# A two-layer decoder trunk on one core: one weight pool for all layers, output projections through the seven-product pair, evacuations queued ahead of the casts that reuse a slot

## The chip, the cores and the metric

The kernel runs on 1 core of a Trainium2 chip. It is timed in device microseconds, from the start to the end of one execution, and the number that counts is the median of several runs. TensorE multiplies; VectorE and ScalarE prepare its operands and take its results; GpSimd does some elementwise work; the SyncE queue issues nearly all loads.

## The reference, cut to what matters

For a sequence of 256 positions and a width of 2048, two layers are computed in float32:

```python
for layer in range(2):
    h = rms_norm(x, mix_norm[layer])
    mix = ssd_mla_mixer(h, ...) if layer == 0 else stick_breaking_mixer(h, ...)
    x = x + mix
    h = rms_norm(x, ffn_norm[layer])
    x = x + (silu(h @ w_gate) * (h @ w_up)) @ w_down     # hidden width 5632
return rms_norm(x, final_norm)
```

The mixer of layer 0 is a Mamba-2 scan (SSD, 4 groups of 8 heads) beside latent attention (MLA, 4 groups of 4 heads). Their outputs, 2048 wide each, are joined and multiplied by one output matrix of 4096 x 2048. The mixer of layer 1 is stick-breaking attention (4 groups of 4 heads) with an output matrix of 2048 x 2048. Each of the three 2048 x 2048 products that end a mixer is called an output projection here: two in layer 0 (`uT` of the SSD, `oT` of MLA), one in layer 1 (`oT` of stick-breaking).

## The kernel before, in words

**Exact products.** TensorE multiplies in a reduced float32 format, so every operand is split into a high part (a cast on ScalarE, L251) and a low part (source minus high part, on VectorE, L252). A product is three matmuls: high x high, low x high, high x low. The activations stand transposed, 128 of the contraction at a time; a matmul has 128 rows and 512 columns. Weights arrive as tiles of 128 x 4 x 512 floats (1 MB), and splitting them is most of what VectorE and ScalarE do.

**Plain projection** (`project`, L337 to L363). For each of 4 column blocks of 512, over 16 contraction blocks and 2 halves of the sequence: 16 x 2 x 3 = 96 matmuls into two of four PSUM banks (L345 to L347). All input projections, the output projections and `w_down` run so.

**Seven-product pair** (`pair`, L470 to L556), for gate and up only. The first half of the contraction of two column blocks is done as a 2 x 2 block product with seven products instead of eight (sums of weight blocks at L470, sums of activation blocks in `block_operands`, L430 to L450, 12 matmuls each at L499, L500 and L504), the second half directly (L532 to L534). One running bank collects four of the seven products and is copied out between them (`keep`, L510; differences at L515). A pair has 7 x 12 + 96 = 180 matmuls, where two plain column blocks have 192. The eight weight tiles of a pair become eleven split parts, and four sums of 128 x 2048 are formed on VectorE.

**Buffers.** In the mixers ("acts" region) there are three weight tiles, and split parts of two contraction blocks (128 x 1024), four of each. In the FFN ("sums" region) there are four weight tiles, split parts of four contraction blocks (128 x 2048), three of each, and two tiles for sums. The two regions share one space, and `region` (L88) closes one before it opens the other, so the first split parts of an FFN reuse the space of the last parts and operands of a mixer. All else that is small comes from a pool of 42 tiles of 128 x 512 (`s2`).

**Order.** TensorE's instructions run in the order in which the program writes them. Side work (attention heads, transposes) is written as generators that say after how many ticks they go on; a tick passes with every six matmuls or so. On the other engines a scheduler fixes the order ahead of the run, by a priority number: casts of weights count up from 100000, adds to the residual and copies out of a running bank have 50000 (`URGENT`), most else ten million. Each engine then works through its queue in that order; an instruction that waits holds up those behind it.

**SSD groups** (`ssd_group`, L943 to L998). Each of the four groups transposes its part of x (L975), scales it (L976, L977), lets GpSimd form `xd` (L980) and after a `yield 3` has TensorE multiply it (L983). GpSimd also multiplies the decay masks (L967, four a group) and adds the last term of the group before (L998).

## Time and profile before

| what | value |
|---|---|
| median of 3 runs | 2491.4 us (2491.02 to 2493.19) |
| the profiled execution | 2491.61 us, span 2489.9 us, 28071 instructions |
| TensorE busy, matmuls | 2438.8 us, 98% of the span |
| VectorE busy | 1739.2 us, 70% |
| ScalarE busy | 1324.8 us, 53% |
| loaded from HBM | 450.85 MB, 182 GB/s over the span |

The profile is one execution. "Busy" is the time in which an engine had an instruction in work; matmuls overlap, so the rate at which they start says more than their busy time. "Idle before" is the time in which an engine stood still ahead of an instruction, with the releaser whose semaphore came last. The weight loads of TensorE (PEld) run under the matmuls. In the first 750 us lie the mixer of layer 0 and the first pairs of its FFN; this FFN ends near 1350 us, the stick-breaking mixer near 1764 us, and the FFN of layer 1 fills the rest.

### The profile page before, as it was taken

To read this page: it belongs to the slowest core of one execution; us is meant where nothing else is said; L and a number is where in the kernel's file an instruction comes from. 1 tells how busy PE (TensorE), PEld (TensorE's weight loads), DVE (VectorE), ACT (ScalarE), POOL (GpSimd) and SP (SyncE) were. 2 spreads that over 40 slices of the span, in tenths; PEclk is the share of its full clock that TensorE was granted. 3 is DMA by queue.
4 is the path that set the end of the run, shared out by engine and by line. 5 is a ranking of instruction groups with operands and counts; after the bars stand their busy time and mean duration, and the time that the engine had idled before them with its cause. 6 is when DMAs were issued, how large, how long until landed. Compare 5 with 4: busy or idle time off the path is not lost.

```text
span 2489.9 us, 28071 instructions
## 1 busy us (share of the span) xinstructions
PE 2438.8 (98%) x11176; PEld 2008.5 (81%) x11176; DVE 1739.2 (70%) x1631; ACT 1324.8 (53%) x1421; POOL 127.7 (5%) x165
## 2 busy tenths in 40 slices
PE   8989999999899999999999999999999999999998
PEld 7777887788778888888878888888778888888877
DVE  6776555546777878787984555556777878787874
ACT  6655555434554545454654456564554545554553
POOL 1342121000000000000000000000000000000001
PEclk9999999999999999999999999999999999999999
DMA  7554553355465656565654555555555656565653
GB/s 236 187 168 136 183 163 111 119 186 186 168 215 175 220 177 224 174 209 196 204 202 152 183 161 163 169 170 184 178 195 184 217 173 221 170 234 170 237 188 117
DMA packets 257828, 454.81 MB, mean 183 GB/s; under 512 B 20716, under 2 KB 45424, under 8 KB 257696
## 3 DMA queue, kind: packets, MB, share of 16 engines
q1 hardware_dynamic: 255168, 446.48, 54.3%
q0 software_dynamic: 1952, 5.48, 0.7%
q8 instruction: 88, 1.44, 0.2%
q10 hardware_dynamic: 576, 1.05, 0.1%
q14 instruction: 44, 0.36, 0.0%
HBM read 450.85 MB, written 2.13 MB: 182 GB/s over the span
## 4 chain that ended last, share of the span: by engine, by line
PE 60%; issue 34%; DVE 3%; POOL 1%; DMA 1%; ACT 1%; SPq 0%; POOLq 0%; ACTq 0%; DVEq 0%
PE acc L345 13%; PE acc L347 13%; PE acc L346 13%; PE acc L532 3%; PE acc L534 3%; PE acc L533 3%; PE acc L499 2%; PE acc L500 2%; PE acc L504 2%; DVE wl L252 1%; PE tr L261 1%; PE at L1062 1%; POOL s L967 1%; ACT wh L251 1%; PE at L991 1%
## 5 line engine op out<-in xcount | busy, mean ns | idle before, releaser
L252 DVE TENSOR_TENSOR wl<-w,wh 128x1024 fp32r<-128x1024 f32 (+2 forms) x586 | 997.7, 1709 | 553.1 <-ACT wh L251 549.1
L251 ACT CAST wh<-w 128x1024 fp32r<-128x1024 f32 (+2 forms) x586 | 837.1, 1430 | 788.2 <-PE acc L347 531.9
L345 PE MATMUL acc<-wh,s 128*128 128x512 f32 (+1 forms) x1728 | 692.2, 401 | 0.6 <-ACT wh L251 0.6
L346 PE MATMUL acc<-wl,s 128*128 128x512 f32 (+1 forms) x1728 | 671.5, 389 | 1.8 <-DVE wl L252 1.7
L347 PE MATMUL acc<-wh,s 128*128 128x512 f32 (+1 forms) x1728 | 672.4, 389 | 0.0
L347 PEld LDWEIGHTS acc<-wh,s 128*128 128x128 f32 x1728 | 325.4, 188 | 68.9
L346 PEld LDWEIGHTS acc<-wl,s 128*128 128x128 f32 x1728 | 326.5, 189 | 66.0 <-DVE wl L252 2.8
L345 PEld LDWEIGHTS acc<-wh,s 128*128 128x128 f32 x1728 | 326.4, 189 | 63.6 <-issue 2.4
L534 PE MATMUL acc<-wl,s 128*128 128x512 f32 x704 | 274.1, 389 | 0.0
L532 PE MATMUL acc<-wh,s 128*128 128x512 f32 x704 | 273.9, 389 | 0.0
L533 PE MATMUL acc<-wh,s 128*128 128x512 f32 x704 | 273.9, 389 | 0.0
L499 PE MATMUL acc<-wh,s 128*128 128x512 f32 x616 | 245.4, 398 | 0.0
L500 PE MATMUL acc<-wh,s 128*128 128x512 f32 x616 | 242.2, 393 | 0.0
L504 PE MATMUL acc<-wl,s 128*128 128x512 f32 x616 | 166.9, 393 | 12.3 <-DVE wl L252 12.3
L251 ACT CAST wh<-wsum 128x2048 fp32r<-128x2048 f32 x66 | 126.4, 1915 | 87.3 <-PE acc L533 33.7
L252 DVE TENSOR_TENSOR wl<-wsum,wh 128x2048 fp32r<-128x2048 f32 x66 | 150.7, 2286 | 13.5 <-ACT wh L251 13.5
L534 PEld LDWEIGHTS acc<-wl,s 128*128 128x128 f32 x704 | 132.1, 188 | 28.2 <-DVE wl L252 0.8
L533 PEld LDWEIGHTS acc<-wh,s 128*128 128x128 f32 x704 | 132.1, 188 | 27.4
L532 PEld LDWEIGHTS acc<-wh,s 128*128 128x128 f32 x704 | 132.1, 188 | 27.4
L504 PEld LDWEIGHTS acc<-wl,s 128*128 128x128 f32 x616 | 115.7, 189 | 39.2 <-DVE wl L252 15.3
L499 PEld LDWEIGHTS acc<-wh,s 128*128 128x128 f32 x616 | 117.8, 191 | 23.6
L500 PEld LDWEIGHTS acc<-wh,s 128*128 128x128 f32 x616 | 117.4, 191 | 23.5
(247 smaller groups left out, 2057.8 us busy)
## 6 DMA issues: line engine op xcount, KB each, us to landing
w<-in_w_gate_dram SPq DMA_DIRECT2D x88, 1024.0 KB, 5.1
w<-in_w_up_dram SPq DMA_DIRECT2D x88, 1024.0 KB, 5.1
w<-in_w_down_dram SPq DMA_DIRECT2D x88, 1024.0 KB, 5.0
w<-in_w_qkv_dram SPq DMA_DIRECT2D x48, 1024.0 KB, 5.0
w<-in_w_in_dram SPq DMA_DIRECT2D x47, 1024.0 KB, 5.1
w<-in_w_out_even_dram SPq DMA_DIRECT2D x32, 1024.0 KB, 4.9
w<-in_w_out_odd_dram SPq DMA_DIRECT2D x16, 1024.0 KB, 4.9
w<-in_w_ukv_dram SPq DMA_DIRECT2D x32, 256.0 KB, 3.8
```

The costliest lines, as they stand in the source:

```text
L251: nc.scalar.copy(hi, src)
L252: nc.vector.tensor_tensor(lo, src, hi.bitcast(F32), op=ALU.subtract)
L261: self.nc.tensor.transpose(pt[:, k, t * P:(t + 1) * P], src(t, 2 * k2 + k), self.ident)
L345: nc.tensor.matmul(ps[t], hi[:, ts], wh, start=k == 0, stop=False)
L346: nc.tensor.matmul(ps[t], hi[:, ts], wl, start=False, stop=False)
L347: nc.tensor.matmul(ps[t], lo[:, ts], wh, start=False, stop=k == nk - 1)
L499: mm(ps, hi[:, k], wh[:, k], start=start and k == 0, stop=False, skip_group_check=True)
L500: mm(ps, lo[:, k], wh[:, k], start=False, stop=False, skip_group_check=True)
L504: mm(ps, hi[:, k], wl[:, k], start=False, stop=k == 3, skip_group_check=True)
L532: mm(ps, hi, wh, start=False, stop=False, skip_group_check=True)
L533: mm(ps, lo, wh, start=False, stop=False, skip_group_check=True)
L534: mm(ps, hi, wl, start=False, stop=stop, skip_group_check=True)
```

## The change

1. **One weight pool.** Weight tiles (4) and split parts (3 of each, 128 x 2048) come from one pool in all layers. The shared space is left with `s2x` (8 tiles) and, from the SSD's output projection on, the two tiles for sums; it changes once, inside layer 0. Other tiles move to the pool of 42.
2. **Output projections through the pair.** `project_residual` replaces `project` and `add_residual`: two pairs for each output projection, each of which ends in adds to the residual. For the SSD the blocks 0 and 1 are made into seven operands by `operand_block`; for MLA and stick-breaking the head outputs of groups 0 and 1 are kept as unsplit blocks, from which `operand_ready` makes the operands. The signs of the sums change, the number of products and sums in a pair does not. Each bank's tile of a pair now runs its eight high-weight matmuls before its four low-weight ones. The first pair of MLA's and of stick-breaking's projection has the order `LATE`.
3. **Evacuations in the queue.** `urgent()` gives copies out of PSUM priority 50000 and notes them with the number of the part; the casts of a part three or more later are queued behind them (`after_urgent`).
4. **Ticks.** Several waits of the side work change: 3 to 6 in an SSD group, 6 to 7 and 3 to 4 in an MLA head, 2 to 8 and 4 to 8 elsewhere. The FFN's operands wait 15 ticks.

The core of the diff:

```diff
+    @contextmanager
+    def urgent(self):
+        traced = self.nc.cur_bb.bb.instructions
+        keep, self.tc.cur_priority = self.tc.cur_priority, self.URGENT
+        last = traced[-1]
+        yield
+        self.tc.cur_priority = keep
+        n = next(k for k in reversed(range(len(traced))) if traced[k] is last) + 1
+        self.pressing.extend((self.parts, ins) for ins in traced[n:]
+                             if ins.engine in (mybir.EngineType.Activation, mybir.EngineType.DVE))
+    def after_urgent(self):
+        order = ExitStack()
+        for part, ins in self.pressing:
+            if part <= self.parts - 3:
+                order.enter_context(self.tc.issue_after(ins))
+        self.pressing = [p for p in self.pressing if p[0] > self.parts - 3]
+        return order
...
-        return self.xp.tile([P, *shape], dt, name=self.nm("s2x"), tag="s2x", bufs=20)
-    def wtile(self):
-        self.wn += 1
-        pool, bufs = (self.xp, 1) if self.shared_kind == "sums" and self.wn % 4 == 0 else (self.wp, 3)
-        return pool.tile([P, 4, 512], F32, name=self.nm("w"), tag="w", bufs=bufs)
-    def part(self, tag):
-        nk, bufs = (2, 4) if self.shared_kind == "acts" else (4, 3)
-        return self.xp.tile([P, nk, 512], F32R, name=self.nm(tag), tag=tag, bufs=bufs)
+        return self.xp.tile([P, *shape], dt, name=self.nm("s2x"), tag="s2x", bufs=8)
+    def wtile(self, tag="w", dt=F32, bufs=4):
+        return self.wp.tile([P, 4, 512], dt, name=self.nm(tag), tag=tag, bufs=bufs)
+    def part(self, tag):
+        return self.wtile(tag, F32R, 3)
...
+    MIXED = ("M1", "M3", "M5", "M2", "M6", "M4", "M7", "c0", "c1", "c2", "c3")
+    LATE = ("M1", "M3", "M5", "M2", "M6", "c0", "M4", "M7", "c1", "c2", "c3")
+    def project_residual(self, st, view, scale=None, done=None, order=MIXED):
...
+        for n in (0, 2):
+            self.pair(st, view(n), view(n + 1), add(n), add(n + 1), self.MIXED if n else order)
+            if done:
+                done(n)
+                done(n + 1)
...
     def wsplit(self, w):
         wh, wl = self.part("wh"), self.part("wl")
-        with self.priority(self.wprio):
+        self.parts += 1
+        with self.priority(self.wprio), self.after_urgent():
...
     def stick(self, st):
...
-        for n in range(4):
-            ps = self.project(aT, self.cols(i["w_out_odd"][0], n * 512), KD)
-            self.add_residual(ps, n)
-            if n < 2:
-                self.operand_block(st, n, self.g_ffn[1])
-            else:
-                self.norm_block(st, n, self.g_ffn[1], rank=self.URGENT)
+        self.project_residual(oT, lambda n: self.cols(i["w_out_odd"][0], n * 512), None,
+                              lambda n: self.norm_next(st, n, self.g_ffn[1]), self.LATE)
...
         nc.gpsimd.tensor_tensor(v3(xd), v3(xdt[0]), bc(self.edec[:, 0, hs]), op=ALU.mult)
-        yield 3
+        yield 6
```

What it moves is shown at three places, each before and after. **GpSimd in the second SSD group**: `s_233` to `s_236` (after: `s_197` to `s_200`) are the masks, `s2x_185` (after: `s_30`) takes the last term of the group before, and the last row is `xd`.

```order
L967 TENSOR_TENSOR s_233_1194<-s_233_1194,s_182_918 128x512
L998 TENSOR_TENSOR s2x_185<-s2x_185,s_249_1318 128x512
L967 TENSOR_TENSOR s_234_1196<-s_234_1196,s_182_918 128x512
L967 TENSOR_TENSOR s_235_1198<-s_235_1198,s_184_932 128x512
L967 TENSOR_TENSOR s_236_1200<-s_236_1200,s_184_932 128x512
L980 TENSOR_TENSOR s_262_1397<-s2x_178,edec_819 128x512
```

```order
L1036 TENSOR_TENSOR s_197_1132<-s_197_1132,s_158_880 128x512
L1036 TENSOR_TENSOR s_198_1134<-s_198_1134,s_158_880 128x512
L1036 TENSOR_TENSOR s_199_1136<-s_199_1136,s_160_894 128x512
L1036 TENSOR_TENSOR s_200_1138<-s_200_1138,s_160_894 128x512
L1067 TENSOR_TENSOR s_30_185<-s_30_185,s_216_1280 128x512
L1049 TENSOR_TENSOR s_222_1327<-s2x_178,edec_789 128x512
```

Before, three of the four masks stand between the last term and `xd`; now all four stand ahead of both.

**VectorE where the stick-breaking mixer meets the FFN of layer 1.** Before, the last two adds to the residual and the first rows of the first FFN pair (`wsum` and `w` on the left are sums of weight tiles, `wl` low parts):

```order
L252 TENSOR_TENSOR wl_13101<-w_13094,wh_13100 128x1024
L401 TENSOR_TENSOR xres<-acc_12964,xres 128x512
L401 TENSOR_TENSOR xres<-acc_12965,xres 128x512
L470 TENSOR_TENSOR wsum_13150<-w_13134,w_13136 128x2048
L252 TENSOR_TENSOR wl_13153<-w_13134,wh_13152 128x2048
L470 TENSOR_TENSOR wsum_13156<-wsum_13150,w_13138 128x2048
L470 TENSOR_TENSOR w_13136<-w_13136,w_13138 128x2048
```

After, the end of the second pair of the output projection: `s_2180` to `s_2186` are low parts of the FFN's seven operands, `wl_12641` is the low part of the pair's last tile, `wl_12691` that of the first tile of the first FFN pair:

```order
L526 TENSOR_TENSOR wsum_12687<-w_12673,w_12671 128x2048
L269 TENSOR_TENSOR s_2180_12565<-s_2170_12545,s_2179_12564 128x512
L269 TENSOR_TENSOR s_2182_12569<-s_2171_12546,s_2181_12568 128x512
L526 TENSOR_TENSOR wsum_12688<-w_12675,wsum_12687 128x2048
L444 TENSOR_TENSOR s_2143_12387<-acc_12359,s_2143_12387 128x512
L269 TENSOR_TENSOR s_2184_12573<-s_2147_12402,s_2183_12572 128x512
L425 TENSOR_TENSOR xres<-s_2143_12387,xres 128x512
L444 TENSOR_TENSOR s_2167_12514<-acc_12360,s_2167_12514 128x512
L269 TENSOR_TENSOR s_2186_12577<-s_2172_12547,s_2185_12576 128x512
L425 TENSOR_TENSOR xres<-s_2167_12514,xres 128x512
L269 TENSOR_TENSOR wl_12641<-w_12346,wh_12640 128x2048
L269 TENSOR_TENSOR wl_12691<-w_12671,wh_12690 128x2048
```

The operands and two sums of the next pair now stand ahead of the last low part of the pair in work. From the row behind the first low part of this pair (`wl_12352`) up to and with `wl_12641` the queue has 42 rows: 14 of 128 x 2048 and 28 of 128 x 512.

**TensorE at the end of MLA's first output pair.** The last head's transposes (L1153) and its last product (L1159, L1160) stand close ahead of the tile that needs the head's split (`s_817` to `s_820`); before, its rows had a whole further projection (that of the SSD) behind them.

```order
L559 MATMUL acc_4470<-wh_4755,s_725_4076 128x512
L1159 MATMUL at_4779<-s_888_4742,s_815_4435 128x256
L1160 MATMUL at_4779<-s_888_4742,s_816_4437 128x128
L1153 MATMUL tr_4784<-ident,s_880_4698 128x128 x3
L559 MATMUL acc_4470<-wl_4756,s_722_4073 128x512 x2
L559 MATMUL acc_4470<-wl_4756,s_724_4075 128x512 x2
L1159 MATMUL at_4798<-s_894_4788,s_815_4435 128x256
L1160 MATMUL at_4798<-s_894_4788,s_816_4437 128x128
L559 MATMUL acc_4471<-wh_4794,s_817_4439 128x512
```

Four matmuls are left between the transposes and the product that needs their copy.

370 lines of the change are left out of this document (202 added, 168 removed).

## The prediction

> **What bounds the kernel now.** I read the busy shares first, then the chain of waits in order of time, then a table of stretches by stage, then who waited for whom.
>
> ```profile
> core 0 of [0], span 2489.9 us
> PE 2438.8 (98%) x11176; PEld 2008.5 (81%) x11176; DVE 1739.2 (70%) x1631; ACT 1324.8 (53%) x1421; POOL 127.7 (5%) x165
> ...
> 1911.46 0.91 PE acc L504 x4
> 1914.18 0.91 PE acc L504 x4
> ```
>
> TensorE is busy almost throughout. The last two rows give its rate: they are the ends of two products of 12 matmuls that follow one another in a steady FFN pair, 2.72 us apart, so 0.227 us a matmul. While it runs at that rate only fewer matmuls help. What else can be had lies where it does not, and the stretches show where. After the two ends of a stretch come its length, then busy time of TensorE, weight load, VectorE, ScalarE and GpSimd, then granted clock.
>
> ```profile
> 1906.80:1989.40 82.60, 82.60 (x369) 68.24 (x368) 69.80 (x43) 49.66 (x36) 0.00 (x0) 1.00 0.61 204
> 652.40:750.40 98.00, 88.72 (x380) 71.63 (x380) 83.81 (x60) 57.67 (x49) 0.00 (x0) 0.97 0.54 183
> 1764.30:1862.30 98.00, 89.64 (x377) 72.48 (x376) 83.28 (x59) 57.06 (x48) 0.00 (x0) 0.95 0.57 193
> 116.00:149.20 33.20, 29.84 (x153) 24.26 (x151) 26.60 (x45) 18.98 (x24) 16.54 (x13) 1.00 0.55 181
> 149.20:183.40 34.20, 30.84 (x149) 24.69 (x149) 23.75 (x43) 18.03 (x23) 13.30 (x11) 0.95 0.46 154
> 183.40:217.70 34.30, 30.94 (x149) 24.74 (x149) 23.74 (x43) 18.03 (x23) 13.27 (x10) 0.95 0.46 154
> 217.70:252.00 34.30, 34.30 (x160) 27.78 (x161) 15.69 (x25) 18.08 (x29) 2.20 (x1) 0.95 0.40 126
> ...
> PE acc L504 <- DVE wl L252: 12.3, 6, 3.4
> PE at L983 <- POOL s L980: 10.1, 3, 3.4
> PE tr L261 <- DVE s L575: 9.9, 4, 2.9
> PE acc L346 <- DVE wl L252: 1.7, 1, 1.7
> ```
>
> Two steady pairs take 82.6 us with no idle TensorE (first row). The first two pairs of either FFN take 98.0 us, with VectorE near its limit (83 us of work). In the SSD groups TensorE is idle 3.4 us a group and then runs at a clock of 0.95. The waits (total, times, longest) name both: low weight parts from VectorE at the FFN starts, and `xd` from GpSimd at L983. A wait costs more than itself, as two matmuls just behind one show:
>
> ```profile
> 1779.70 0.63 PE L500 MATMUL acc<-wh,s 128*128 128x512 f32 x1
> 1780.13 0.63 PE L499 MATMUL acc<-wh,s 128*128 128x512 f32 x1
> ```
>
> They start 0.43 us apart, about half the rate.
>
> **The change part by part.** *Fewer matmuls.* An output projection drops from 4 x 96 = 384 matmuls to 2 x 180 = 360; three of them save 72, at 0.227 us **16.3 us**. The rate is that of the same instruction in the FFN, so this term is firm as long as TensorE is fed.
>
> *SSD groups.* The idle times are 33.20 - 29.84, 34.20 - 30.84 and 34.30 - 30.94, in all 10.1 us; the three stretches at 0.95 lose 0.05 x 102.8 = 5.1 us. GpSimd's queue in one such group:
>
> ```profile
> 139.15 2.21 POOL L998 TENSOR_TENSOR s2x<-s2x,s 128x512 f32<-128x512 f32 x1 [0.76 <-DVE s L997]
> 141.33 5.74 POOL L967 TENSOR_TENSOR s<-s,s 128x512 f32<-128x512 f32 x3
> 147.02 2.02 POOL L980 TENSOR_TENSOR s<-s2x,edec 128x512 f32<-128x512 f32 x1
> ```
>
> The three masks between L998 and `xd` take 5.74 us and move ahead of L998; the queue needs to be only 3.4 us earlier. On TensorE I count 60 matmuls from the last product of a group to L983 of the next, before and after, so the longer `yield` alone gives nothing there and the order on GpSimd must do it. Bounds: 0 if the masks come late all the same, **15.2 us** if all goes; I take 15.2, since GpSimd was idle ahead of L998.
>
> *Region change after the first FFN.* The single wait at L346, 1.7 us, stands at the start of stick-breaking, where the old regions were exchanged. One pool removes it: **1.7 us** (0 to 1.7).
>
> *The FFN starts.* 98.0 against 82.6 is 15.4 us, of which some is the 16 transposes of the norm:
>
> ```profile
> 1950.45 0.60 PE tr L261 x4
> ...
> L252 DVE TENSOR_TENSOR wl<-w,wh 128x2048 fp32r<-128x2048 f32 x264 | 602.9, 2295 | 225.2 <-ACT wh L251 225.1
> L252 DVE TENSOR_TENSOR wl<-w,wh 128x1024 fp32r<-128x1024 f32 x310 | 386.6, 1249 | 319.5 <-ACT wh L251 315.6 <-DMA w<-in_w_uq_dram 1.6 <-DMA w<-in_w_ukv_dram 1.5
> ...
> 1777.69 2.28 DVE L252 TENSOR_TENSOR wl<-wsum,wh 128x2048 fp32r<-128x2048 f32 x1
> 1779.88 2.28 DVE L252 TENSOR_TENSOR wl<-w,wh 128x2048 fp32r<-128x2048 f32 x1
> ...
> 140.13 0.68 DVE L976 TENSOR_TENSOR s2x<-tr,dt 128x512 f32<-128x512 f32 x1
> 140.73 0.68 DVE L977 TENSOR_TENSOR s2x<-tr,hp 128x512 f32<-128x512 f32 x1
> ```
>
> At 0.60 us for four, 2.4 us; 13.0 us are lost at each start, 26 us together. Then the first split parts waited for the last tiles of the old region; that cause goes. But the load on VectorE moves forward into the new pairs. The second pair of an output projection has, from behind its first low part to its last, 42 rows on VectorE. Queued back to back the wide ones start 2.19 us apart and the short ones 0.60 us: 14 x 2.19 + 28 x 0.60 = 47.5 us. TensorE gets from the pair's start to the last tile's low part in 7 x 2.72 + 3 x 5.44 + 8 x 0.227 + 16 transposes 2.4 = 39.5 us. So VectorE ends 8.0 us late if both start together. It can be some 5 us ahead (three parts may be buffered), which leaves 3, and it can lose 4 us to waits for casts and loads, which makes 12; I take 9. In the first FFN pair the norm's splits add to a queue without lead: 0 to 5 us, I take 3. That is 12 a site, 3 to 17. At the old starts 9.28 and 8.36 idle us came with 2.9 and 4.9 us of lost clock (0.03 and 0.05 of 98), 0.44 a us; for shorter stalls I take a little less, so 14 us a site. Against the 13.0 that go: **+2 us** for the two sites, from -20 to +24.
>
> By a rule of the Trainium skill this factor would fall: "TensorE: Matmul & The Clock Gate", section "What's actually happening", says that the clock halves only after an idle window of about 3.4 us. If the new stalls are all shorter, a site costs 12 and, as an estimate by this page, the sum falls by 4 us. The row at 1779.70 came after waits of 3.4 and 1.9 us, so it does not decide that.
>
> *MLA's tail.* The last head's transposes are followed by four matmuls (0.9 us), then by the product that needs their copy, then by a tile that needs the split of that product:
>
> ```profile
> L1081 ACT COPY s<-tr 128x384 f32<-128x384 f32 x16 | 7.6, 474 | 0.0
> L251 ACT CAST s2x<-at 128x256 fp32r<-128x256 f32 x32 | 11.8, 370 | 9.1 <-PE at L1086 8.7 <-PE at L681 0.2
> L252 DVE TENSOR_TENSOR s2x<-at,s2x 128x256 fp32r<-128x256 f32 x32 | 13.4, 419 | 2.5 <-ACT s2x L251 2.0
> L251 ACT CAST wh<-w 128x2048 fp32r<-128x2048 f32 x264 | 504.8, 1914 | 433.1 <-PE acc L347 221.4 <-PE acc L533 109.0 <-issue 38.6
> ```
>
> Copy, cast and low part are 1.3 us, and each can find one wide cast ahead of it (1.9 us). Between 0.4 us (1.3 less the cover) and 6: **+3 us**.
>
> *The SSD's own pairs.* Here a pair has 15 wide rows and about 13 short ones: 32.9 + 7.8 = 40.7 us on VectorE against 180 x 0.227 = 40.8 on TensorE; 0 to 6, I take **+1.5 us**. The cover is the lead that VectorE brings from the input projections; without it both pairs lose about 3 each.
>
> *Wider casts.* In the mixers a cast on VectorE becomes 2.29 us long instead of 1.25, so an attention step can start 1.05 us later. An MLA head has one tick more at two such steps (six matmuls, 1.36 us each), which covers it there; I take **+2 us**, from 0 to 25 (8 groups with 3 such steps each). In all 302 of the shorter casts become 151 long ones, 0.2 us cheaper per pair, which VectorE has no use for off the path: nothing.
>
> Steady FFN pairs keep their counts and sizes: nothing, covered by 12.8 us of VectorE slack in two pairs.
>
> Sum: -16.3 - 15.2 - 1.7 + 2 + 3 + 1.5 + 2 = -24.7. From the span of 2489.9 that is 2465.2; the profiled execution took 2491.61, 1.7 more than its span, and the median is 0.2 below it: **2467 us**.
>
> **The rivals.** *A, the deficit is hidden.* If VectorE enters the second pairs with its full lead and loads never wait, the sites cost nothing (-28), nor do tail, SSD pairs and casts (-6.5): 2432 us. For it: VectorE is only 70% busy over all. Against it: 47.5 us of queue in a place of 39.5.
>
> *B, L983 waits on.* GpSimd's masks need VectorE and ScalarE first, and those now carry longer casts. The 15.2 us stay: 2482 us.
>
> *C, the wide casts cause bubbles.* Eight attention groups with three uncovered steps lose 25 us instead of 2: 2490 us, no change. Against it: the listed waits of TensorE contain almost nothing from these stages. "Perfetto Trace Analysis" of the Trainium skill, section "Optimizing Scalar/DVE Operations", speaks for C: where these engines are not saturated and yet cause bubbles elsewhere, it advises to break instructions up, the opposite of what is done here.
>
> *D, slower: VectorE bounds all six new pairs.* Place: the queue of VectorE from the first low part of each pair on. Price: 17 in each second pair of MLA and stick-breaking, 9 in each first one (attention's last steps share the queue), 6 in each SSD pair, 5 in each first FFN pair: 34 + 18 + 12 + 10 = 74 us before any clock loss. What goes is 16.3 + 15.2 + 1.7 + 26 = 59. So 2491.4 + 15 = 2506 us; it decides from an average of 7.4 us in each of these eight pairs. For it: the two FFN starts already show what a full VectorE does to TensorE.
>
> **How the numbers follow.** My forecast, with its own range of 2452 to 2478, gets 0.52; A 0.20, B 0.08, C 0.08, D 0.10, something else 0.02. The range of 2430 to 2489 takes in A's and B's times, the bounds of the sites and most of C, and leaves out A's better end and D. About 0.2% (5 us) is what a measurement of this kernel can tell from no change. Faster: the forecast, A, B and a part of C, 0.84; same 0.06; slower 0.10.
>
> **What would show it.** Right: 72 fewer matmuls; no row of L1052 waiting for GpSimd; two SSD groups near 29 to 31 us at full clock; TensorE waiting for low parts in the second output pair of MLA and stick-breaking and in the first FFN pair behind it, 10 to 15 us a site. Wrong: a site with over 25 us or none, waits spread over the attention stages, or VectorE idle while TensorE waits for it, which would make a load or an order the cause.

## The result and the profile after

The changed kernel takes 2460.2 us (median; 2457.5 to 2463.0). The kernel before, run beside it, took 2492.3. The ratio is 0.987, with a 95% interval of 0.9853 to 0.9888: faster by 1.3%. The forecast was 2467 us, in a range of 2430 to 2489, so the time is right. Several terms of the sum are not: they err by 4 to 14 us in both directions, and that they cancel in part is luck.

The head of the page of the changed kernel, in the form in which the prediction showed that of the kernel before:

```profile
span 2458.5 us, 27627 instructions
...
PE 2419.7 (98%) x11104; PEld 1991.0 (81%) x11104; DVE 1837.9 (75%) x1561; ACT 1344.2 (55%) x1337; POOL 136.9 (6%) x165
```

There are 72 fewer matmuls, and VectorE has 98.7 us more work. The stretches of the changed kernel come next (length, then busy time of TensorE, weight load, VectorE, ScalarE and GpSimd, then granted clock): three SSD groups, the end of MLA with its first output pair, the rest of MLA's output projection with the first FFN pairs, the same for stick-breaking, a steady pair of FFN pairs, and a group of three FFN pairs.

```profile
120.40:149.50 29.10, 29.10 (x149) 23.93 (x148) 22.31 (x40) 17.34 (x19) 14.37 (x12) 1.00 0.66 225
149.50:178.60 29.10, 29.10 (x149) 23.92 (x148) 21.63 (x40) 17.56 (x19) 13.25 (x10) 1.00 0.57 187
178.60:207.20 28.60, 28.60 (x145) 23.53 (x144) 21.09 (x40) 18.28 (x23) 11.13 (x6) 1.00 0.51 165
...
500.00:600.00 100.00, 92.18 (x443) 70.89 (x442) 77.17 (x105) 52.76 (x89) 10.30 (x12) 1.00 0.37 126
600.00:733.00 133.00, 129.27 (x575) 105.77 (x574) 120.72 (x96) 84.18 (x84) 0.00 (x0) 0.99 0.54 188
1690.00:1837.00 147.00, 142.39 (x630) 115.78 (x629) 133.29 (x108) 89.99 (x87) 0.00 (x0) 0.98 0.53 186
...
1877.20:1959.80 82.60, 82.60 (x370) 68.42 (x369) 69.74 (x43) 49.80 (x37) 0.00 (x0) 1.00 0.61 204
1154.70:1279.00 124.30, 124.30 (x557) 102.93 (x556) 108.48 (x67) 74.85 (x56) 0.00 (x0) 1.00 0.59 203
```

The SSD groups run at full clock without idle TensorE; from one L1052 to the next they take 29.1, 29.1 and 28.6 us, where the groups before took 32.6, 34.3 and 34.2. The steady pairs are unchanged at 82.6. At both FFN starts VectorE is busy for 91% of the stretch (120.72 of 133.00 and 133.29 of 147.00). TensorE is idle most at the end of MLA, 7.8 us in 100. Who waited (total, times, longest):

```profile
PE acc L559 <- DVE wl L269: 6.0, 7, 3.1
PE at L769 <- DVE s L304: 3.9, 2, 3.3
...
PE at L1159 <- ACT s L1155: 2.8, 3, 1.4
...
PE tr L278 <- DVE xres L425: 2.5, 2, 2.0
PE acc L559 <- DVE s L269: 2.4, 1, 2.4
...
PE at L1135 <- DVE s L1120: 1.3, 1, 1.3
```

No row of L1052 waits for GpSimd. Low parts (L559 <- L269) are late where the prediction put them, and three things are new: stick-breaking's scores wait for copies of transposed q and k (L769 <- L304), and two steps of MLA's heads are late (L1159, and `s` L269 at L559).

For a finer count I take, over a stretch, each gap between the starts of two matmuls and add up what exceeds its usual length (0.227 us behind a matmul of 512 columns). I call this **lost time**; it holds waits and half-speed matmuls alike. By it the kernel before lost 83.6 us in all and the changed one 66.0. What is usual for a short matmul is a matter of choice, by some microseconds in such a total and by one or two in a stage with many short ones; the stages of long matmuls hardly depend on it, and differences between kernels by some 1.5 us.

### The profile page after: what moved, and what is told of

Read it like the earlier page. It is cut to its first block, busy times and chain, and to the rows that moved or that the text cites. A ratio compares the mean times of both kernels' runs of the same rounds, so it can differ in the third digit from the quotient of the medians.

```text
span 2458.5 us, 27627 instructions
## 1 busy us (share of the span) xinstructions
PE 2419.7 (98%) x11104; PEld 1991.0 (81%) x11104; DVE 1837.9 (75%) x1561; ACT 1344.2 (55%) x1337; POOL 136.9 (6%) x165
## 4 chain that ended last, share of the span: by engine, by line
PE 88%; DVE 7%; issue 2%; ACT 1%; DMA 1%; SPq 0%; ACTq 0%; DVEq 0%
PE acc L559 39%; PE acc L361 14%; PE acc L363 14%; PE acc L362 14%; DVE wl L269 4%; PE tr L278 1%; DVE wsum L526 1%; ACT wh L268 1%; PE at L1060 1%; PE at L1136 1%; PE tr L302 0%; DVE w L526 0%; DVE s L269 0%; PE at L1135 0%; DVE s L444 0%
## 5 line engine op out<-in xcount | busy, mean ns | idle before, releaser
L269 DVE TENSOR_TENSOR wl<-w,wh 128x2048 fp32r<-128x2048 f32 (+2 forms) x431 | 967.9, 2256 | 391.3 <-ACT wh L268 387.9
L268 ACT CAST wh<-w 128x2048 fp32r<-128x2048 f32 (+2 forms) x431 | 804.7, 1876 | 537.2 <-PE acc L363 312.7
L559 PE MATMUL acc<-wh,s 128*128 128x512 f32 x3360 | 842.7, 392 | 5.8 <-DVE s L269 2.4
L559 PEld LDWEIGHTS acc<-wh,s 128*128 128x128 f32 x3360 | 628.1, 188 | 137.0 <-ACT s L612 3.6
L361 PE MATMUL acc<-wh,s 128*128 128x512 f32 (+1 forms) x1600 | 637.7, 399 | 0.6 <-ACT wh L268 0.6
L363 PE MATMUL acc<-wh,s 128*128 128x512 f32 (+1 forms) x1600 | 622.1, 389 | 0.0
L559 PE MATMUL acc<-wl,s 128*128 128x512 f32 x1680 | 453.0, 391 | 6.2 <-DVE wl L269 6.0
L559 PEld LDWEIGHTS acc<-wl,s 128*128 128x128 f32 x1680 | 314.6, 188 | 77.9 <-DVE wl L269 12.9
L363 PEld LDWEIGHTS acc<-wh,s 128*128 128x128 f32 x1600 | 301.0, 188 | 63.4
L361 PEld LDWEIGHTS acc<-wh,s 128*128 128x128 f32 x1600 | 301.7, 189 | 57.7 <-issue 1.2
L269 DVE TENSOR_TENSOR wl<-wsum,wh 128x2048 fp32r<-128x2048 f32 x84 | 192.0, 2297 | 15.1 <-ACT wh L268 15.0
L526 DVE TENSOR_TENSOR wsum<-w,wsum 128x2048 f32<-128x2048 f32 x56 | 128.6, 2297 | 9.9 <-DMA w<-in_w_up_dram 7.9
L612 ACT COPY s<-acc 128x512 f32<-128x512 f32 x112 | 65.7, 586 | 103.8 <-PE acc L559 103.8
L526 DVE TENSOR_TENSOR wsum<-w,w 128x2048 f32<-128x2048 f32 x28 | 64.7, 2312 | 8.2 <-DMA w<-in_w_up_dram 5.6
L526 DVE TENSOR_TENSOR w<-w,w 128x2048 f32<-128x2048 f32 x28 | 64.4, 2299 | 0.0
L425 DVE TENSOR_TENSOR xres<-acc,xres 128x512 f32<-128x512 f32 x76 | 51.4, 689 | 10.9 <-PE acc L363 10.3
```

What stands on the lines that cost most here:

```text
L268: nc.scalar.copy(hi, src)
L269: nc.vector.tensor_tensor(lo, src, hi.bitcast(F32), op=ALU.subtract)
L361: nc.tensor.matmul(ps[t], hi[:, ts], wh, start=k == 0, stop=False)
L363: nc.tensor.matmul(ps[t], lo[:, ts], wh, start=False, stop=k == nk - 1)
L425: nc.vector.tensor_tensor(xs, c, xs, op=ALU.add)
L526: self.nc.vector.tensor_tensor(o, p, q, op=ALU.subtract)
```

## The experiments

Each ratio below is to the kernel before, run beside it, with its 95% interval. Line numbers shift by a few between kernels. The times of the kernel before that stand beside the experiments differ by up to 2.6 us (2491.3 to 2493.9), so differences of a few us between experiments are good to about that.

### One wait in the SSD groups, alone and taken back

```diff
         nc.gpsimd.tensor_tensor(v3(xd), v3(xdt[0]), bc(self.edec[:, 0, hs]), op=ALU.mult)
-        yield 3
+        yield 6
```

In the kernel before:

> The kernel before with one number changed: in each SSD group the wait between the scaling of xd on GpSimd and the matmul that reads it (L983) is 6 ticks instead of 3. Nothing else of the change is in it. Theory (the order of GpSimd's queue decides): since the tail of a group is then issued later, its last term (L998) stands behind all four masks of the next group (L967) in GpSimd's queue, xd comes some 2 us or more earlier, and the 10.1 us of waits at L983 and the 5.1 us of clock behind them go: 2492.3 - 15.2 = 2477 us, between 2474 and 2481. Rival (the masks are late all the same, because VectorE and ScalarE feed them): L983 keeps 8 us or more of waits and the time stays at 2489 to 2494.

Measured: 2476.9 us, ratio 0.9933 (0.9918 to 0.9948). GpSimd's order became the one shown of the changed kernel, no wait at L983 is left, and the stretches read like those of the changed kernel:

```profile
121.50:150.60 29.10, 29.10 (x149) 23.92 (x148) 23.31 (x45) 18.03 (x23) 12.10 (x11) 1.00 0.63 209
```

The reverse, in the changed kernel (`yield 6` back to `yield 3`):

> The changed kernel with that wait back at 3 ticks, so that the last term of a group (L1067) stands ahead of three of the next group's masks (L1036) again. Theory (the order of GpSimd's queue decides): TensorE waits for xd again in three groups, 8 to 10 us, with some clock behind it: 2460.2 + 8 to 15 = 2468 to 2475 us. Rival (the waits went because y moved out of the shared pool and VectorE has fewer instructions there): no row of waits at L1052, 2458 to 2463 us.

Measured: 2481.6 us, ratio 0.9952 (0.9937 to 0.9966), 21 us above the changed kernel and more than the 2468 to 2475 that the theory gave. The wait is back, and the clock falls again behind it:

```profile
PE at L1052 <- POOL s L1049: 12.2, 4, 3.1
```

```profile
151.70:185.60 33.90, 30.91 (x148) 24.68 (x148) 21.27 (x39) 17.13 (x19) 12.90 (x11) 0.95 0.50 155
```

So this one number is worth 17 us in the kernel before and 21 in the changed one: it moves the tail of a group, and with it GpSimd's last term, behind the next group's masks. The 12.2 us of waits with their clock make 18 us more lost time in this stage; the rest is spread over the stages behind.

### The queue order of evacuations, taken out

```diff
     def after_urgent(self):
         order = ExitStack()
         for part, ins in self.pressing:
-            if part <= self.parts - 3:
+            if False:
                 order.enter_context(self.tc.issue_after(ins))
```

> The changed kernel without the ordering of casts behind evacuations: evacuations keep their priority, but no cast is held back until they are queued (after_urgent orders nothing). TensorE's order is unchanged. Theory of the prediction, which gave this edit no price: 2460.2 within 5 us. Rival (this ordering is what took the waits out of the third pairs of the two groups of three, 2.5 and 2.7 us before and 0.2 each in the changed kernel, and out of other places where a bank's evacuation stands behind wide casts): both third pairs lose 2 us or more again, other pairs wait for evacuations as well, and the time is 2466 to 2480 us.

Measured: 2525.6 us, ratio 1.0128 (1.0113 to 1.0143), 65 us above the changed kernel and 1.3% slower than the kernel before. The rival is right in its direction, but it claimed too little (2466 to 2480), and not where it looked first: the third FFN pairs lose 1.4 and 1.5 us, under its 2. The largest of TensorE's waits that the changed kernel does not have in this size:

```profile
PE acc L559 <- ACT s L612: 19.3, 8, 4.5
PE acc L363 <- DVE s L269: 10.5, 8, 1.3
PE tr L278 <- DVE s L636: 7.8, 10, 1.6
```

ScalarE's own waits tell why. First the changed kernel, then this one:

```profile
ACT wh L268 <- PE acc L559: 192.5, 70, 9.3
ACT s L612 <- PE acc L559: 103.8, 94, 1.7
```

```profile
ACT wh L268 <- PE acc L559: 336.6, 195, 5.3
...
ACT s L612 <- PE acc L559: 17.0, 11, 1.7
```

L612 copies the running bank out between products, and TensorE cannot write to that bank until it is done. In the changed kernel the copy stands ready at the head of ScalarE's queue and waits for TensorE (94 times). Without the order a cast stands there instead, waiting for its slot (195 times), and the copy behind it is late: 11 times only did it wait for TensorE itself. Whether the wider parts make this worse was not tested. Lost time rises most around the first two output projections: 41 us between 480 and 760 us, where the changed kernel loses some 20, and 20 us between 240 and 430, where it loses some 5.

### Plain output projections

```diff
-        for n in (0, 2):
-            self.pair(st, view(n), view(n + 1), add(n), add(n + 1), ...)
+        aT = self.pairs(st["xT"])
+        for n in range(4):
+            ps = self.project(aT, view(n), KD)
+            for t in range(2):
+                self.add_tile(t, ps[t], n, scale() if scale else None)
```

(with all operand tiles of the three projections split as before, and the FFN's operands no longer queued behind the copies that only a pair makes)

> The changed kernel with its three output projections done as before, by four plain projections of 96 matmuls each (360 back to 384, 72 matmuls more in all), with all their operand tiles split into high and low parts; one weight pool, the wide casts, the GpSimd order and the ordering of evacuations stay. So it tells what the seven-product output projections are worth with all that hangs on them. By the prediction's terms, the projections gave -16.3 for the matmuls, +3 for the end of MLA, +1.5 for the SSD's own pairs, and the two FFN starts cost 28 in the place of 26: without them the matmuls come back, the last two go, and a first FFN pair with a queue of VectorE of its own costs 3 to 5 us a site instead of 14. Theory (the price of the projections is VectorE's queue at the FFN starts): 2460.2 + 16.3 - 4.5 - 18 to -22 = 2450 to 2454 us, so the projections are a net loss of some 8 us. Rival (the sites are lost to the norm's splits and operands, not to the projections): the starts stay at 8 to 13 us each, and the time is 2468 to 2477 us.

Measured: 2449.6 us, ratio 0.9823 (0.9806 to 0.9839): 10.6 us faster than the changed kernel, with 72 more matmuls. The theory forecast 2450 to 2454. TensorE's waits, all of 0.5 us or more:

```profile
PE at L1148 <- ACT s L1144: 2.8, 3, 1.7
PE tr L236 <- DMA s<-in_mix_norm_dram: 2.7, 1, 2.7
PE tr L1142 <- DVE s L1138: 2.6, 1, 2.6
PE tr L278 <- DMA xres<-in_x_dram: 2.5, 1, 2.5
PE acc L361 <- ACT wh L268: 0.8, 1, 0.8
PE at L991 <- ACT s L977: 0.5, 1, 0.5
```

Two of them are the start of the kernel and two the end of MLA; at the FFN starts nothing is left (lost time 0.7 and 2.0 us in stretches of 120 and 190 us). So with plain projections the rest of the change (one pool, the queue orders and the ticks together) leaves nothing of what the FFN starts lost, and the first FFN pair has no deficit of its own. Which of these parts does it was not separated.

### The seven-product projection for the SSD alone

> The changed kernel with plain output projections for MLA and stick-breaking and the seven-product one for the SSD's own projection alone: 24 of the 72 matmuls stay away. The kernel with three plain projections took 2449.6 us. By the lost time of TensorE in its stretches, the SSD's projection costs 2.6 us of waits and gives 24 x 0.227 = 5.4, MLA's costs 9 for 5.4 and stick-breaking's 15 for 5.4. Theory (each projection's balance stands for itself: a gain where no attention and no norm share VectorE with it): 2449.6 - 2.8 = 2446.8 us, between 2444.5 and 2449. Rival (the stalls move on to the next stage, so the matmuls saved give nothing): 2449 to 2453 us.

Its edit is that of the last experiment, for MLA and stick-breaking only. Measured: 2447.2 us, ratio 0.9813 (0.9797 to 0.983), where the sum of the separate balances gave 2446.8. In the changed kernel the seven products of stick-breaking and MLA together cost more than they save; where no attention and no norm shares VectorE, they are worth having. The difference to all-plain, 2.4 us, is near what can be told apart, and rests on the lost time (3.5 against 0.4 us in the stage, for 5.4 us of matmuls).

### Four tests of what is late at the FFN starts

**Less work for VectorE** in the second output pairs:

```diff
-        self.wsub(t1, raw["b12"], raw["b11"])
...
+        if sums:
+            self.wsub(t1, raw["b12"], raw["b11"])
+        else:
+            t1 = t2 = raw["b12"]
```

> The changed kernel without the four weight sums in the second output pairs of MLA and of stick-breaking: the products there read loaded weights where they should read sums, so these two projections compute something else. All loads, casts and matmuls stay; VectorE has 4 x 2.3 = 9.2 us less in each of these two pairs, which is a little more than the 8.0 us by which the prediction had it end late. Theory (VectorE's queue in that pair): the waits of 1.45 us (634), 2.1 (642) and 3.25 us (1735) and the half speed behind the last go, and the FFN pairs behind begin with a lead: 2460.2 - 7 to -13 = 2447 to 2453 us. Rival (the loads come late there): nothing changes, 2458 to 2463 us.

Measured: 2454.0 us, ratio 0.9844 (0.9829 to 0.9858): 6.2 us off, a little under the 7 to 13 that were expected. The wait at 1735 us fell from 3.25 to 1.4 and the half speed behind it is gone, but a wait of 2.0 us for an add to the residual (L425) came up behind it, at 1743. At MLA's site nothing changed: 1.45 us at 634 and 2.0 at 642 stayed. So VectorE's work in the second pair is the cause at one site of the two.

**Another order of the same work.** VectorE's queue in the changed kernel shows what stands ahead of the awaited low part:

```profile
1727.20 2.29 DVE L526 TENSOR_TENSOR wsum<-w,w 128x2048 f32<-128x2048 f32 x1
1729.41 1.29 DVE L269 TENSOR_TENSOR s<-s,s 128x512 fp32r<-128x512 f32 x2
1730.62 2.28 DVE L526 TENSOR_TENSOR wsum<-w,wsum 128x2048 f32<-128x2048 f32 x1
...
1736.42 4.49 DVE L269 TENSOR_TENSOR wl<-w,wh 128x2048 fp32r<-128x2048 f32 x2
```

The L526 rows are sums for the next pair, the first of the FFN; the first of the two in the last row is what TensorE waits for. So I queued these sums behind it (`issue_after` the last low part, ahead of both FFNs):

> The changed kernel with the order of VectorE's queue changed at two places: the three weight sums of the first FFN pair (L526, 2.3 us each) are queued behind the last low part of the output projection before it. In the changed kernel two of them stand ahead of that low part, which TensorE awaits for 1.45 us (634) and 3.25 us (1735), although its cast was done 7 us earlier at the second place. Theory (the queue's order, with some 2.2 us of other work, makes this wait, not the amount of work): both waits go, and with them the half speed behind the second: 2460.2 - 5 to -8 = 2452 to 2455 us. Rival (VectorE is short there whatever the order): the sums come late in their turn, the first FFN pair waits for the low parts of the sums by about as much, 2457 to 2464 us.

Measured: 2462.9 us, ratio 0.9881 (0.9863 to 0.9898). The rival is right. The waits at 634 and 1735 are gone, and in their place TensorE waits 2.7 and 3.2 us at 644 and 657, 2.7 and 2.6 us at 1747 and 1761, in the first FFN pair:

```profile
PE acc L566 <- ACT wh L269: 7.0, 3, 3.0
PE acc L566 <- DVE wl L270: 5.2, 3, 2.5
```

Lost time in the two stretches is 10.5 and 10.7 us instead of 6.8 and 9.5. So the operands, the sums and the low parts around the FFN start are more than VectorE can do in time there, at both sites, and this order only moves the place where TensorE waits for them.

**The operands on GpSimd.** `eng` is GpSimd at the FFN starts:

```diff
-        nc.vector.tensor_tensor(s1, a21, a22, op=ALU.add)
+        eng.tensor_tensor(s1, a21, a22, op=ALU.add)
...
-            self.split(hi, lo, a)
+            nc.scalar.copy(hi, a)
+            eng.tensor_tensor(lo, a, hi.bitcast(F32), op=ALU.subtract)
```

> The changed kernel, but at the two FFN starts the four sums and the seven low parts of the FFN's operands (11 instructions of 128x512) are done by GpSimd, which is idle there, instead of VectorE, and are begun 9 ticks earlier, since GpSimd needs some 2 us for each. In the changed kernel the last tile of stick-breaking's second output pair waits 3.25 us for its low part at 1735 us, and MLA's second pair waits 1.45 us at 634. Theory (VectorE's queue is too long there): 11 x 0.6 = 6.6 us less of it takes both waits away, with the half-speed matmuls behind the first, some 6 to 9 us: 2460.2 - 6 to -9 = 2451 to 2454 us. Rival (a load or a cast is late, not VectorE): the waits stay and the time is 2458 to 2463 us. Second rival: GpSimd is too slow, or slows VectorE beside it: TensorE waits for operands at the first FFN pair, 2463 to 2475 us.

Measured: 2468.0 us, ratio 0.9898 (0.9883 to 0.9913), 8 us slower than the changed kernel, as the second rival said, but through another engine. ScalarE and GpSimd at the place:

```profile
1722.01 0.62 ACT L505 CAST s<-s 128x512 fp32r<-128x512 f32 x1 [2.68 <-POOL s L498]
1725.28 0.62 ACT L505 CAST s<-s 128x512 fp32r<-128x512 f32 x1 [2.65 <-POOL s L498]
1725.80 0.58 ACT L614 COPY s<-acc 128x512 f32<-128x512 f32 x1
```

```profile
1717.05 8.19 POOL L498 TENSOR_TENSOR s<-s,s 128x512 f32<-128x512 f32 x3
```

Each sum takes GpSimd 2.7 us. ScalarE's casts of the sums wait for them at the head of its queue, and behind them stands the copy of the running bank (L614): TensorE waits 4.4 us for it. The wait for low parts did get shorter (longest 1.9 us instead of 3.1), so VectorE was relieved; the chain through GpSimd cost more.

**The copies of q and k first**, and then both orders together:

```diff
             o = self.s2([2, S])
-            self.nc.vector.tensor_copy(o, pt)
+            with self.urgent():
+                self.nc.vector.tensor_copy(o, pt)
```

> The changed kernel, but the copies of transposed q and k (L304 on VectorE, 32 in the kernel) are queued ahead of casts in the way that evacuations are. In the changed kernel TensorE waits 3.45 us for one of them at 1631 us and then runs at half speed for some 2 us; two more short waits for such copies stand at 524 and 1626 us. Theory (this wait is a copy behind wide low parts and sums of the first output pair, the price of wider instructions that the prediction put into the attention steps): it goes, 2460.2 - 4 to -7 = 2453 to 2456 us. Rival (the low parts that the copies are put ahead of then come late themselves, and the wait moves to the first output pair): 2458 to 2464 us.

Measured: 2457.0 us, ratio 0.9854 (0.984 to 0.9869), 3.2 us less than the changed kernel, at the edge of what can be told apart, and between the two forecasts. The waits at L769 are gone, and the lost time between 1600 and 1680 us falls from 8.1 to 3.1. The low part at the FFN start is 0.3 us later in exchange (longest wait 3.4).

> The changed kernel, with all three seven-product projections, and with both orders: the first FFN pair's sums behind the last low part of the output projection, and the attention's copies and softmax queued ahead of casts. Theory (most of what MLA's and stick-breaking's projections lose is a matter of order on VectorE and ScalarE): 2460.2 - 3.2 (copies, as measured) - 5 to -8 (sums) - 2 to -4 (MLA's last heads) = 2445 to 2450 us, as good as plain projections there. Rival (it is the amount of VectorE's work: in these pairs 47.5 us of queue stand against 39.5 of TensorE): 2453 to 2460 us, some 8 us behind the kernel that keeps them plain.

Here the MLA softmax and the copies of probabilities were made urgent too. Measured: 2463.1 us, ratio 0.9881 (0.9866 to 0.9897): above both forecasts, and no better than the sums' order alone. Neither order, nor both, brings the three projections to the time of one. The tail of MLA did not gain: the waits for copies of probabilities are gone, but the product behind the last head now waits 5.6 us for its split in one piece. The cast of that split ended at 579.3, and its low part (0.42 us) began only at 585.0, behind a low part and two sums of the second output pair. This split was not among the steps that were put ahead, so an order that would help here was left untried.

### The end of MLA

Two kernels with the seven-product projection for the SSD alone. In one, MLA's and stick-breaking's steps go ahead of casts, by the edit just described:

> The kernel with the seven-product projection for the SSD alone (2447.2 us), and with the attention's copies of transposed q, k and probabilities and the MLA softmax on VectorE and ScalarE queued ahead of casts as evacuations are. That kernel's TensorE still waits 2.6 us for the scaling of probabilities and 2.8 us in three places for their transposed copy at MLA's last heads (560 to 570 us). Theory (these steps stand behind 2.3 us low parts and 1.9 us casts): 2447.2 - 3 to -5 = 2442 to 2444 us. Rival (they are late by their own chain of four engines' steps, which no order shortens): 2446 to 2449 us.

Measured: 2446.3 us, ratio 0.9812 (0.9796 to 0.9827): no gain that can be told, and the waits at MLA's end stand unchanged at 2.6 and 2.8 us. With plain projections, order is not their cause. TensorE in the kernel without this edit, in that place:

```profile
556.04 0.70 PE L1152 MATMUL at<-s,s 128*128 128x256 f32 x2 [1.66 <-ACT s L1148]
...
565.48 0.87 PE L1146 MATMUL tr<-ident,s 128*128 128x128 f32 x3 [2.56 <-DVE s L1142]
566.92 1.22 PE L1152 MATMUL at<-s,s 128*128 128x256 f32 x2 [0.57 <-ACT s L1148]
```

There is no projection between the steps of the last heads: scores, softmax, transpose and product follow one another, and TensorE waits for each. So the other kernel puts work there:

```diff
+        for i, k0, k1 in ((0, 0, 12), (1, 0, 12), (0, 12, 16), (1, 12, 16)):
+            for k in range(k0, k1):
+                wh, wl = next(gens[i])        # weights of column block i
+                hi, lo = xT(k)
...
+            if k1 == KD:
+                yield ps[i]
```

> The kernel with the seven-product projection for the SSD alone (2447.2 us), and with the first two column blocks of MLA's and of stick-breaking's plain output projection interleaved: three quarters of the contraction of both (24 ticks), then the last quarter of both, which alone needs the outputs of the last four heads. Number and kind of all instructions stay. In that kernel TensorE runs the last heads of MLA with nothing between their steps from 554 to 568 us, because the first column block needs them after 12 ticks and the last head takes 25; before the change the SSD's output projection stood there. Theory (MLA's tail is a lack of cover on TensorE, since the SSD's projection was moved ahead of MLA): the waits of 5.3 us and the half speed around them go, 2447.2 - 7 to -10 = 2437 to 2440 us. Rival (the tail is late because of wide casts and low parts on ScalarE and VectorE): the waits move along with the heads and the time stays at 2444 to 2449 us.

Measured: 2437.7 us, ratio 0.9783 (0.9766 to 0.9799). It is the fastest of all, 22.5 us below the changed kernel, and 9.5 below the kernel without the interleaving (7.5 by the two ratios, 0.9783 against 0.9813). The same stage, first without and then with the interleaving:

```profile
554.00:572.00 18.00, 12.64 (x41) 8.71 (x40) 5.32 (x11) 4.93 (x12) 0.00 (x0) 0.62 0.19 58
```

```profile
540.00:590.00 50.00, 50.00 (x239) 40.03 (x238) 25.31 (x38) 21.14 (x33) 0.00 (x0) 1.00 0.44 148
```

Idle time and half speed are both gone, with the same instructions. Before the change the SSD's output projection stood behind MLA and gave this cover (in the kernel before, no wait of TensorE is listed between 250 and 655 us); the change moved it ahead of MLA. The cover was tested with plain projections alone. In the changed kernel a seven-product pair stands between the last heads, and its waits have another cause, as the rows of ScalarE and VectorE ahead of the waits at 580 and 582 us show:

```profile
578.15 1.91 ACT L268 CAST wh<-w 128x2048 fp32r<-128x2048 f32 x1 [3.19 <-issue]
...
580.23 0.48 ACT L1155 COPY s<-tr 128x384 f32<-128x384 f32 x1
```

```profile
582.60 2.28 DVE L526 TENSOR_TENSOR w<-w,w 128x2048 f32<-128x2048 f32 x1
584.80 0.75 DVE L269 TENSOR_TENSOR s<-at,s 128x256 fp32r<-128x256 f32 x2
```

The copy of the last head's probabilities stands behind a wide cast, and the low part of its product, whose cast was done at 582.1, behind a sum of the second output pair.

## Why the prediction was right or wrong

The terms, with the lost time or the stretches that answer to them:

| term | forecast | measured | from |
|---|---|---|---|
| 72 fewer matmuls | -16.3 | -16.3 | count, steady pairs unchanged at 82.6 |
| SSD groups | -15.2 | -14.3 | three groups, 101.1 to 86.8 us |
| region change, L346 | -1.7 | -1.7 | the wait is gone |
| FFN starts | +2 | -12.5 | lost time 14.1 + 14.7 to 6.8 + 9.5 |
| MLA's tail | +3 | about +10.5 | lost 12.1 in 500 to 600; before, 5.9 in the 400 us from 253 to 650, so 1.5 in as long a stretch |
| SSD's own pairs | +1.5 | +2.6 | lost 3.0, against 0.4 when plain |
| wider casts in attention | +2 | about +6 | lost 6.7 in 1600 to 1650, against 0.7 with plain projections and casts as wide |
| groups of three FFN pairs | none | -4.6 | lost 2.7 + 2.9 to 0.4 + 0.6 |

They add up to -30.3 us; the span fell by 31.4. Since lost time at MLA's end depends most on the choice of the usual length, its row is the least firm; idle time there is 7.8 us of 100, and none of it is in the kernel before.

**The matmuls and the SSD groups: right.** These two make most of the gain. The SSD term rested on the sentence that the longer `yield` alone gives nothing and GpSimd's order must do it. The order does it, but the longer `yield` is what makes that order, as its two experiments show; so the one-line edit is worth the whole term. Rival B (L983 waits on) is refuted.

**The FFN starts: mechanism right at one site, size wrong at both.** TensorE waits for the last low part of the second output pair, as forecast. At stick-breaking it does so for the forecast reason: VectorE has no pause from 1684 us to the awaited low part at 1736, and four sums fewer take 1.8 us off the wait. At MLA it does not: VectorE had caught up within the pair (four pauses, 4.4 us together, between 585 and 613 us), four sums fewer changed nothing, and the low part stands behind the operands and sums of the first FFN pair alone. No late load or cast is involved: the cast of that tile was done some 8 us earlier at both sites. The term that was mis-sized is the 14 us a site: they lost 6.8 and 9.5, normal gaps included, so the sign of 10 to 15 us a site was not met. Of its parts, the 3 us for a first FFN pair "without lead" are not there: with plain projections it loses nothing. VectorE's late end was taken as 9 us and shows as 1.5 and 3.3 us of waiting for low parts, with the adds to the residual (2.0 us, L425) queued there. For lost clock the old starts had given 0.44 us a us of wait; the step from 12 to 14 us used 0.17, which is less than half of that and not "a little less". At 1735 us it was 0.8: 13 matmuls at half speed behind 3.25 us, some 2.7 us. The Trainium skill's rule that was weighed there ("TensorE: Matmul & The Clock Gate", "What's actually happening": the clock halves after an idle window of about 3.4 us) did not spare these sites.

**MLA's tail: part of the cost was left out.** I priced copy, cast and low part of the last head behind four matmuls at 0.4 to 6 us and took 3. This step is there as priced: 2.4 us for the low part at 582 us, behind wide work in VectorE's queue. What the sum left out is the rest of the heads. Copies of probabilities of earlier heads come late too (L1159, 2.8 us in three waits, two of them behind wide casts). And making the seven operands out of the head outputs of groups 0 and 1 holds up two steps, the third of those waits at 520 us and one of 1.3 us at 525 (L1135): seven casts stand on ScalarE from 515.5 to 521.3 us and six low parts on VectorE from 521.6 to 525.2. The move of the SSD's projection has a price of its own, which the sum did not have either, although the rows shown ahead of the prediction say that this projection stood behind the heads before: with plain projections, too, 10.0 us are lost from 500 to 600 us, and giving that place other work takes the lost time from 480 to 600 us from 11.6 to 2.8. How much of the changed kernel's own loss cover would remove was not tested.

**Wider casts: the wrong cause.** The cost lies at one place and not in every step: stick-breaking's last scores wait 3.3 us for a copy of transposed q and k. On VectorE the copy stands behind two sums of the first output pair:

```profile
1628.79 2.49 DVE L526 TENSOR_TENSOR wsum<-w,wsum 128x2048 f32<-128x2048 f32 x1
1631.21 2.48 DVE L526 TENSOR_TENSOR w<-w,w 128x2048 f32<-128x2048 f32 x1
1633.62 0.68 DVE L304 COPY s<-tr 128x512 f32<-128x512 f32 x1
```

The experiment with urgent copies removes the wait. So do plain projections, which keep the wide casts and have no sums; so it belongs to the seven-product projection, and the term for wider casts itself comes out near nothing there. Rival C (25 us of bubbles over the stages) is refuted. What "Perfetto Trace Analysis" of the Trainium skill ("Optimizing Scalar/DVE Operations") advises, to break instructions up, was not tried; at stick-breaking's scores an earlier place in the queue removed the wait, and at MLA's end with plain projections cover on TensorE did.

**What the sum left out.** The queue order of evacuations got no price, since I looked for what it gains over the kernel before. It carries the change: without it the time is 2525.6 us. The 4.6 us in the groups of three were not foreseen either: before, TensorE waited in each third pair for the gated product of the second (2.2 us in the first group, L261 for L575). Without the queue order these groups lose 1.4 and 1.5 us, with it 0.4 and 0.6, before 2.7 and 2.9: 1.9 us of the 4.6 are the order, and what the other 2.7 are stays open.

**Rival D** (VectorE bounds all six pairs, slower) had the right engine and too high a price: the second output pairs cost a fraction of its 17 us each. What it says of the first pairs, that attention's last steps share VectorE's queue with them, is what happened at 1631 us. And its direction holds for the projections taken alone: those of MLA and stick-breaking lose 13 us together (2460.2 against 2447.2), and the kernel is faster because other edits pay for them.

## What to carry to other kernels

An edit that saves matmuls on the bounding engine is worth its saving only where the engines that feed it have slack at that place: here 24 matmuls fewer were a gain of about 2 us in one place, near what can be told apart, and a loss in two others taken together. When a step is moved, ask what it was covering: the moved projection had hidden a chain of dependent steps, and giving other work to that place was worth 9.5 us where putting the same steps ahead in the queues gave nothing that can be told. Whatever releases TensorE must stand in each queue ahead of work that waits for a slot: without this one order the changed kernel takes 65 us more.

## What the runs showed of the hardware that was not expected

Half speed came after waits shorter than I had reckoned with, and not after every one. In the changed kernel it follows the wait of 3.1 us at 1735 and one of 2.0 us at 642, but not one of 2.4 us at 582. The granted clock (last but two in the row) shows why. It falls to half for stretches of 3.41 us or multiples of it, and within a run all of them begin on one grid of 3.41 us. Cut on this grid, the places look so:

```profile
580.71:584.12 3.41, 2.07 (x9) 1.46 (x9) 3.41 (x2) 0.37 (x1) 0.00 (x0) 1.00 0.72 241
584.12:587.54 3.42, 2.27 (x10) 1.89 (x11) 1.77 (x4) 0.00 (x0) 0.00 (x0) 1.00 0.82 299
642.15:645.56 3.41, 1.44 (x11) 1.18 (x10) 3.41 (x5) 1.06 (x3) 0.00 (x0) 1.00 0.38 112
645.56:648.97 3.41, 3.41 (x13) 2.92 (x12) 3.41 (x4) 2.48 (x6) 0.00 (x0) 0.50 0.80 286
1737.82:1744.65 6.83, 5.89 (x14) 4.62 (x15) 5.94 (x4) 0.36 (x1) 0.00 (x0) 0.50 0.65 233
```

The wait at 582 is split between two of these windows, which have 1.34 and 1.15 us of idle TensorE; the one at 642 lies in one window, with 1.97 us, and the next window runs at half clock. Over the traces of all 14 kernels here, behind the first 30 us, each of the 53 windows at full clock with 2.0 us of idle TensorE or more was followed by one at half clock, 10 of the 20 with 1.7 to 2.0 us were, and 3 of some 2800 with less. Inside half clock 0.5 us of idle time was enough to keep it for another window, in all 29 cases. The Trainium skill ("TensorE: Matmul & The Clock Gate", "What's actually happening") gives one idle window of about 3.4 us, and says that the window runs freely. The grid agrees with the length and with the second; but a window need not be idle throughout, some 2 us of it were enough. So a wait of 2 to 3 us halves the clock or not by where it falls on the grid. And several short waits can do what a long one does: at MLA's end in the kernel with the seven-product projection for the SSD alone, waits of 1.66 and 0.57 us put 1.8 us of idle time into one window, and half clock followed for 13.7 us (0.62 over the 18 us shown above), although no single wait there was over 2.6 us.
